# Fourteen of 22 pairs of activation tiles in the down projection by seven products instead of plain ones, in two groups of seven pairs

## The chip, the cores and the metric

The kernel runs on one core of a Trainium2 chip. The metric is the device time of one execution in microseconds; lower is better. The times named are medians of several runs, and the profile comes from one further execution.

## The reference

One encoder layer over two requests of 256 tokens each (512 tokens, 2048 features), in float32: a mixer of neighbourhood attention and a gated delta rule, then a gated feed-forward network, then a last RMS norm. The change is in the feed-forward network's last product:

```python
h = h + mixed
hn = rmsnorm(h, norm_ffn_w)
return h + (jax.nn.silu(hn @ w_gate) * (hn @ w_up)) @ w_down
```

`w_gate` and `w_up` are 2048 x 5632, `w_down` is 5632 x 2048. The 5632 inner features are 44 tiles of 128, or 22 pairs.

## The kernel before

**Precision.** A float32 operand is split in a high and a low part (`split`, L125 on): ScalarE copies the high part (L130), VectorE subtracts it (L131). A plain product is three matmuls of 512 columns: high by high, high by low, low by high (`mm3`).

**Gate and up, by seven products.** `block` (L964) makes a 2 x 2 block of output tiles: two tiles of features by two halves of tokens, from two halves of the inner dimension. It computes Strassen's seven products instead of eight. Each product (L933) runs over 8 tiles of the inner dimension with two matmuls each, one of 512 columns (the high weight by the high and the low part of 256 tokens) and one of 256 (the low weight by the high part). The combinations of activations are made once, ahead of the stage, and lie in the seven slots of `XC`. The combinations of weights are made per block: `second` is w12 + w22 and `first` is w11 + w12, each loaded by SP and then added to by an accumulating DMA on GpSimd's queue (`plus`, L960). `first` is split for the third product; then VectorE adds b22 (L1010) and it is split for the fifth; then VectorE adds b21 (L1022) and it is split for the seventh. `b11`, `b21` and `b22` are loaded again by themselves. The split weights `hi` and `lo` have three buffers, so a split runs up to two products ahead. The pools of `first` and `second` are `gA` for a gate block and `gB` for an up block, one buffer each. The results of the seven products are summed by VectorE from PSUM. After each pair of blocks the activations go to DRAM (`s_act`, L1063), except for the pairs of one segment, which stay on chip in `sA`.

**Down, plain.** A segment is two pairs, four tiles of the inner dimension. `load_act` (L1083) reads a pair of activation tiles from `s_act` and splits it. `down` (L1091) runs, for each of 8 output columns of 256 features, over the segments of a group of tiles on chip: 24 matmuls of 512 columns per segment and column, and at the end VectorE adds PSUM into the residual stream `hT` (L1102), which has been loaded whole from `s_h2`. The segments go in groups: 9 (from `sA`), then 0 to 2, then 3, 4, 5 and 10, then 6 and 7. The last segment, 8, runs by halves of tokens with the final norm beside it (`finish`, `final_norm`).

**Order.** A scheduler orders the instructions of the engines other than TensorE by its own costs; TensorE keeps the order of the program. `high_priority(offset=...)` lets loads and splits be placed ahead. Each engine runs its queue in order, and so do SP and GpSimd with the DMAs that they issue.

Of the kernel before, what the change touches and what calls it, by code (L numbers as in the profile page):

```python
# [18 lines left out]
P = 128  # L19
# [13 lines left out]
FIRST_SEG = 9  # L33
# [32 lines left out]
def hybrid_encoder(ctx: ExitStack, tc: tile.TileContext, xT, w_in, w_ba, w_out, w_gate,  # L66
                   w_up, w_down, nw_mix, nw_ffn, nw_fin, na_bias, conv_w, lane_par,
# [865 lines left out]
    def product(ps, w, c, first, done=False):  # L933

        wh, wl = w
        for k in range(8):
            mm(ps, wh[:, k], XC[k][:, c], start=(first and k == 0), stop=False,
               skip_group_check=True)
            mm(ps[:, 0], wl[:, k], XC[k][:, c, 0], start=False, stop=(done and k == 7),
               skip_group_check=True)  # L940
# [10 lines left out]
    def w_split(src):  # L951
        hi = wp.tile([P, 8, P], F32R, tag="hi", bufs=3, name="w_hi")
        lo = wp.tile([P, 8, P], F32R, tag="lo", bufs=3, name="w_lo")
        split(hi, lo, src)
        return hi, lo
# [8 lines left out]
    def block(src, f, pool, new_out, opened=None):  # L964


        with tc.high_priority(offset=3 * AHEAD):
            first = pool.tile([P, 8, P], F32, tag="first", name="w_first")
            second = pool.tile([P, 8, P], F32, tag="second", name="w_second")
            nc.sync.dma_start(second, src[f + 1, 0])  # L970
            nc.sync.dma_start(first, src[f, 0])
            plus(second, src[f + 1, 1])
            plus(first, src[f + 1, 0])
            b11, b21, b22 = [wp.tile([P, 8, P], F32, tag="raw", bufs=3, name=nm)
                             for nm in ("b11", "b21", "b22")]
            nc.sync.dma_start(b11, src[f, 0])
            nc.sync.dma_start(b21, src[f, 1])
            nc.sync.dma_start(b22, src[f + 1, 1])
# [8 lines left out]
        product(pa, w, A11, True)  # L987
# [3 lines left out]
        p1 = gA.tile([P, L], F32, tag="p1", name="p1")  # L991
# [3 lines left out]
        product(pc, w, S3, True)  # L995
# [4 lines left out]
        product(pd, w, S1, True)  # L1000
        if opened:
            token_rstd2()
        d = fp.tile([P, 2, L], F32, tag="d", name="d")
        tt(d, pd, p7, ALU.subtract)
        with ahead():
            w = w_split(b21)
        product(pa, w, A12, False, True)
# [4 lines left out]
        product(pb, w, S2, True, True)  # L1012
        u2 = fp.tile([P, L], F32, tag="u2", name="u2")
        plus_both(u2, p1, pb)
        tt(out[:, 3], d[:, 0], u2, ALU.subtract)
        tt(out[:, 3], out[:, 3], d[:, 1], ALU.add)
        with ahead():
            w = w_split(b22)
        product(pd, w, S4, False, True)
# [4 lines left out]
        product(pc, w, A22, False, True)  # L1024
        plus_both(out[:, 1], u2, pc)
        a = out.rearrange("p (f b) t -> p f (b t)", f=2)
        tt(a, a, state["rstd2"][:, None, :].broadcast_to([P, 2, T]), ALU.mult)
        return out

# [7 lines left out]
    def open_gate():  # L1037
# [3 lines left out]
                                                 reuse_waits="tile"))  # L1041
        state["gb_cm"] = tc.tile_pool(name="gB", bufs=1, side="right", reuse_waits="tile")
# [3 lines left out]
        state["sA"] = sA_pool.tile([P, 2, SEG, T], F32R, tag="sA", name="aA")  # L1046

    for p in range(NPAIR):
        g4 = block(w_gate, 2 * p, gA,
                   lambda: state["fp"].tile([P, 4, L], F32, tag="g4", name="ga"),  # L1050
                   open_gate if p == 0 else None)
        act(out=g4, in_=g4, func=AF.Silu)
        u4 = block(w_up, 2 * p, state["gB"],
                   lambda: state["fp"].tile([P, 4, L], F32, tag="u4", bufs=2, name="up"))
# [26 lines left out]
    qp = ctx.enter_context(tc.tile_pool(name="qp", bufs=1, side="right", reuse_waits="tile"))  # L1081

    def load_act(s, a):  # L1083

        for i in range(2):
            raw = fp.tile([P, 2 * T], F32, tag="raw_a", name="raw_a")
            nc.gpsimd.dma_start(raw, s_act[2 * s + i])
            split(a[:, 0, 2 * i:2 * i + 2].rearrange("p k t -> p (k t)"),
                  a[:, 1, 2 * i:2 * i + 2].rearrange("p k t -> p (k t)"), raw)

    def down(segs):  # L1091
        for j in range(8):
            ps = [pg.tile([P, T], F32, tag="g", name="ps_g"), sm_tile()]
            for n, (s, a) in enumerate(segs):
                wh, wl = load_w(w_down[s, j], [2, SEG, P])
                for i in range(2):
                    for k in range(SEG):
                        mm3(ps[i], wh[:, i, k], wl[:, i, k], a[:, 0, k], a[:, 1, k],
                            n == 0 and k == 0, n == len(segs) - 1 and k == SEG - 1)
            for i in range(2):  # L1100
                hk = hrow(2 * j + i)
                tt(hk, hk, ps[i], ALU.add)  # L1102

    def down_half(s, aseg, t0, t1, keep):
        for j in range(8):
            wh, wl = keep[0][:, j], keep[1][:, j]
            if t0 == 0:
                load_w(w_down[s, j], [2, SEG, P], (wh, wl))
# [9 lines left out]
    def final_norm(b, acc):  # L1118
# [8 lines left out]
        dgs = fp.tile([P, 2, P], F32, tag="raw_a", name="dgs")  # L1127
# [5 lines left out]
        yo = qp.tile([P, KT, L], F32, tag=f"q{b}", name="yo")  # L1133
        for k, n in ((0, 2), (2, 2), (4, 4), (8, 4), (12, 4)):
            tt(yo[:, k:k + n], hT[k // 8][:, k % 8:k % 8 + n, t0:t1],
               rs[:, None, :].broadcast_to([P, n, L]), ALU.mult)
            nc.sync.dma_start(y[b, k // 4, :, k % 4:k % 4 + n], yo[:, k:k + n])
# [115 lines left out]
```

## Time and profile before

| | |
|---|---|
| median of 3 runs | 2338.44 us (2337.36 to 2339.56) |
| the profiled execution | 2336.3 us, its span 2334.4 us |
| granted TensorE clock | 0.998 |
| TensorE busy | 2301.2 us, 99% of the span |
| VectorE, ScalarE, GpSimd busy | 69%, 42%, 9% |
| DMA | 371.08 MB, mean 159 GB/s |

The gate and up blocks end at about 1839 us of the span; the down projection and the final norm fill the rest. The busy time of an engine says how long it had work in flight. A wait is read from the chain of waits and from the bracket at the end of a timeline row, which gives the idle time before an instruction and what ended it.

### The profile page before, as it was taken

The numbers are of one execution on the slowest core, as the hardware profiler recorded it, in microseconds if no ns is written. First come the engines' busy times: TensorE is split into PE (matmuls) and PEld (weight loads), VectorE is DVE, ScalarE is ACT, GpSimd is POOL, SyncE is SP. The second block draws the span as 40 slices with busy tenths as digits, with TensorE's granted clock in tenths as the row PEclk, the third lists the DMA queues.
The fourth block names the chain that finished last, engine by engine and source line by source line (L and its number), as shares of the span: only waits on it lengthen the run. The fifth ranks groups of instructions, "written<-read, shape, count | busy, mean of one in ns | idle before, by whom it ended". The sixth has DMA issues, their size and how long they took to land.

```text
span 2334.4 us, 31279 instructions
## 1 busy us (share of the span) xinstructions
PE 2301.2 (99%) x12092; PEld 1929.3 (83%) x12092; DVE 1615.1 (69%) x2380; ACT 982.7 (42%) x1478; POOL 218.2 (9%) x326
## 2 busy tenths in 40 slices
PE   9999999999999999999999999999999999999998
PEld 7887788888778788888888888888888888888887
DVE  7744799974666636888888888888888753422346
ACT  6777333324333324644444444444444342311225
POOL 2211100011100011100010101010100110000000
PEclk9999999999999999999999999999999999999999
DMA  5434423265434554777777777767676562422231
GB/s 203 133 118 140 121 93 104 95 143 168 127 118 136 193 168 171 219 187 197 202 191 212 190 210 186 218 184 215 184 203 180 208 224 92 135 99 95 95 126 73
DMA packets 105012, 371.08 MB, mean 159 GB/s; under 512 B 13568, under 2 KB 14032, under 8 KB 103584
## 3 DMA queue, kind: packets, MB, share of 16 engines
q1 hardware_dynamic: 74960, 268.21, 33.9%
q0 software_dynamic: 29904, 100.88, 19.2%
q8 instruction: 95, 1.56, 0.3%
q14 instruction: 53, 0.43, 0.1%
HBM read 333.57 MB, written 35.47 MB: 158 GB/s over the span
## 4 chain that ended last, share of the span: by engine, by line
PE 84%; DVE 8%; ACT 4%; issue 2%; DMA 1%; POOL 0%; SPq 0%; DVEq 0%; ACTq 0%; POOLq 0%
PE ps_g L78 33%; PE ps_s L78 12%; PE ps_a L78 11%; PE ps_c L78 11%; PE ps_d L78 10%; PE ps_b L78 5%; DVE w_lo L131 2%; PE ps_o L78 1%; DVE cacc L335 1%; ACT w_hi L130 1%; DVE prod L546 1%; DVE W L548 1%; ACT E L453 1%; PE ps_s L81 1%; ACT E L455 1%
## 5 line engine op out<-in xcount | busy, mean ns | idle before, releaser
L131 DVE TENSOR_TENSOR w_lo<-w_raw,w_hi 128x1024 fp32r<-128x1024 f32 x222 | 271.2, 1223 | 288.4 <-ACT w_hi L130 285.1
L130 ACT ACTIVATE w_hi<-w_raw 128x1024 fp32r<-128x1024 f32 x222 | 234.1, 1057 | 511.3 <-PE ps_s L78 281.7
L78 PE MATMUL ps_g<-xhi,w_hi 128*128 128x512 f32 x896 | 361.6, 404 | 1.4 <-DVE on L423 1.4
L78 PE MATMUL ps_g<-xhi,w_lo 128*128 128x512 f32 x896 | 350.5, 391 | 2.5 <-DVE w_lo L131 2.5
L78 PE MATMUL ps_g<-xlo,w_hi 128*128 128x512 f32 x896 | 350.2, 391 | 0.5 <-DVE xlo L239 0.5
L78 PE MATMUL ps_a<-xc,w_hi 128*128 128x512 f32 x704 | 252.5, 399 | 2.0 <-DVE p L946 1.2
L78 PE MATMUL ps_d<-xc,w_hi 128*128 128x512 f32 x704 | 250.4, 396 | 1.1 <-ACT w_hi L130 1.1
L78 PE MATMUL ps_c<-xc,w_hi 128*128 128x512 f32 x704 | 250.3, 396 | 0.0
L130 ACT ACTIVATE w_hi<-w_first 128x1024 fp32r<-128x1024 f32 x132 | 140.1, 1061 | 204.6 <-PE ps_c L78 109.5
L130 ACT ACTIVATE w_hi<-b 128x1024 fp32r<-128x1024 f32 x132 | 140.2, 1062 | 193.4 <-issue 115.6
L131 DVE TENSOR_TENSOR w_lo<-w_first,w_hi 128x1024 fp32r<-128x1024 f32 x132 | 161.7, 1225 | 75.0 <-ACT w_hi L130 70.9
L78 PEld LDWEIGHTS ps_g<-xhi,w_lo 128*128 128x128 f32 x896 | 168.3, 188 | 39.7 <-DVE w_lo L131 3.9
L78 PEld LDWEIGHTS ps_g<-xhi,w_hi 128*128 128x128 f32 x896 | 168.6, 188 | 38.6 <-issue 5.7
L78 PE MATMUL ps_a<-xc,w_lo 128*128 128x256 f32 x704 | 197.4, 280 | 0.0
L78 PE MATMUL ps_d<-xc,w_lo 128*128 128x256 f32 x704 | 197.3, 280 | 0.0
L78 PE MATMUL ps_c<-xc,w_lo 128*128 128x256 f32 x704 | 197.3, 280 | 0.0
L78 PEld LDWEIGHTS ps_g<-xlo,w_hi 128*128 128x128 f32 x896 | 168.7, 188 | 34.1 <-DVE xlo L239 1.5
L131 DVE TENSOR_TENSOR w_lo<-b,w_hi 128x1024 fp32r<-128x1024 f32 x132 | 161.2, 1221 | 7.6 <-ACT w_hi L130 0.3
L78 PEld LDWEIGHTS ps_a<-xc,w_hi 128*128 128x128 f32 x704 | 132.1, 188 | 38.1 <-issue 5.9
L78 PEld LDWEIGHTS ps_d<-xc,w_hi 128*128 128x128 f32 x704 | 132.1, 188 | 32.6 <-ACT w_hi L130 1.4
L78 PEld LDWEIGHTS ps_c<-xc,w_hi 128*128 128x128 f32 x704 | 132.1, 188 | 31.2
L78 PEld LDWEIGHTS ps_a<-xc,w_lo 128*128 128x128 f32 x704 | 133.1, 189 | 0.3 <-issue 0.2
(336 smaller groups left out, 4312.0 us busy)
## 6 DMA issues: line engine op xcount, KB each, us to landing
w_raw<-in_w_in_dram SPq DMA_DIRECT2D x110, 512.0 KB, 3.5
w_raw<-in_w_down_dram SPq DMA_DIRECT2D x88, 512.0 KB, 3.3
b<-in_w_gate_dram SPq DMA_DIRECT2D x66, 512.0 KB, 4.1
b<-in_w_up_dram SPq DMA_DIRECT2D x66, 512.0 KB, 6.5
w_raw<-in_w_out_dram SPq DMA_DIRECT2D x32, 512.0 KB, 3.5
w_second<-in_w_gate_dram SPq DMA_DIRECT2D x22, 512.0 KB, 8.4
w_first<-in_w_gate_dram SPq DMA_DIRECT2D x22, 512.0 KB, 6.0
w_second<-in_w_gate_dram POOLq DMA_DIRECT2D x22, 512.0 KB, 5.5
```

The lines of the kernel that those rows point to most:

```text
L78: pin(nc.tensor.matmul(*a, **k))
L81: pin(nc.tensor.transpose(*a))
L130: act(out=hi, in_=src, func=AF.Copy)
L131: tt(lo, src, r32(hi), ALU.subtract)
L335: stt(a3[:, :, lo:hi], x3[:, :, lo + o:hi + o], cw[:, ct, j:j + 1], a3[:, :, lo:hi], ALU.mult, ALU.add)
L453: pin(act(out=E[half[0], s, s:], in_=G[half[0], s:], func=AF.Exp, bias=NG[half[0], s:s + 1]))
L455: pin(act(out=E[half[1], s, :s + 1], in_=G[half[1], :s + 1], func=AF.Exp, bias=NG[half[1], s:s + 1]))
L546: tt(pv, W[:, s0:s1, s0:c], kkq[:, c, 0, None, s0:c].broadcast_to([P, n, j]), ALU.mult)
L548: nc.vector.tensor_reduce(W[:, s0:s1, c], pv, AX.X, ALU.add)
```

## The change

The 44 tiles of the down projection are divided anew. Tiles 0 to 27, 14 pairs, form two groups of seven pairs. Each group is multiplied by `block`, now with 7 tiles of the inner dimension in each half instead of 8: the first tiles of the pairs are one half, the second tiles the other. The other four segments stay plain and run one at a time: 9, then the first group, 7, the second group, 8, and 10 by halves at the end.

The combinations of activations for a group, `XD` (seven tiles of seven slots), are made by `combine` from one loaded pair each, one beside each output column of the plain segment that stands ahead of the group. `hT` is no longer loaded whole: in the first segment ScalarE copies PSUM into it, and an accumulating DMA adds `s_h2`. The results of a group's block are added into `hT` by VectorE (L1149 after). All tiles of a group's blocks come from the pool `fq` with one buffer per tag; loaded pairs, combinations and the blocks' outputs share a ring of three buffers. `w_group` holds the weights of the groups.

```diff
+GROUP = 7
+NGROUP = 2
+FIRST_SEG, MID_SEG, LAST_SEGS = 9, 7, (8, 10)
...
-    def block(src, f, pool, new_out, opened=None):
+    def block(w4, pool, xc, ix, p1_pool, new_out, opened=None):
+        n = len(xc)
+        w11, w21, w12, w22 = w4
         with tc.high_priority(offset=3 * AHEAD):
-            first = pool.tile([P, 8, P], F32, tag="first", name="w_first")
-            second = pool.tile([P, 8, P], F32, tag="second", name="w_second")
+            first = pool.tile([P, n, P], F32, tag="first", name="w_first")
+            second = pool.tile([P, n, P], F32, tag="second", name="w_second")
...
-        d = fp.tile([P, 2, L], F32, tag="d", name="d")
-        tt(d, pd, p7, ALU.subtract)
+        tt(p7, pd, p7, ALU.subtract)
...
-        a = out.rearrange("p (f b) t -> p f (b t)", f=2)
-        tt(a, a, state["rstd2"][:, None, :].broadcast_to([P, 2, T]), ALU.mult)
         return out
...
-    for i in range(KT):
-        nc.gpsimd.dma_start(hrow(i), s_h2[i])
-    fp = ctx.enter_context(tc.tile_pool(name="fq", bufs=2, side="left", reuse_waits="tile"))
+    fq = ctx.enter_context(tc.tile_pool(name="fq", bufs=1, side="right", reuse_waits="tile"))
+    XD = [hq.tile([P, 7, 2, L], F32R, tag=f"xd{k}", name="xd") for k in range(GROUP)]
+    ix = (0, 3, 4, 1, 5, 6, 2)
+
+    def ring(shape, nm):
+        return fq.tile([P] + shape, F32, tag="ra", bufs=3, name=nm)
+
+    def combine(p, k):
+        raw, cm, x = ring([4, L], "raw_a"), ring([4, L], "cmd"), XD[k]
+        nc.gpsimd.dma_start(raw.rearrange("p a t -> p (a t)"), s_act[p])
+        tt(cm[:, :2], raw[:, :2], raw[:, 1:4:2], ALU.subtract)
+        tt(cm[:, 2], cm[:, 1], raw[:, 0], ALU.subtract)
+        tt(cm[:, 3], raw[:, 2], cm[:, 2], ALU.add)
+        split(x[:, 0, 0], x[:, 0, 1], raw[:, 0])
+        split(x[:, 1:3, 0], x[:, 1:3, 1], raw[:, 2:])
+        split(x[:, 3:, 0], x[:, 3:, 1], cm)
...
-    def down(segs):
+    def down(s, a, beside=None, first=False):
         for j in range(8):
+            if beside is not None and j < GROUP:
+                combine(beside + j, j)
...
             for i in range(2):
                 hk = hrow(2 * j + i)
-                tt(hk, hk, ps[i], ALU.add)
+                if first:
+                    nc.scalar.copy(hk, ps[i])
+                else:
+                    tt(hk, hk, ps[i], ALU.add)
+            if first:
+                plus(hcol(j), s_h2[2 * j:2 * j + 2].rearrange("i p t -> p i t"))
+
+    def down_group(g):
+        for j in range(8):
+            out = block([w_group[g, j, i] for i in range(4)], fq, XD, ix, fq,
+                        lambda: ring([4, L], "out"))
+            h4 = hcol(j).rearrange("p i t -> p (i t)")
+            tt(h4, h4, out.rearrange("p a t -> p (a t)"), ALU.add)
...
+            yo = out[:, k:k + n] if b else ring([n, L], "yo")
...
+    down(FIRST_SEG, state["sA"], 0, True)
+    a = load_act(MID_SEG, state["new_sA"]())
+    down_group(0)
+    down(MID_SEG, a, GROUP)
+    a = load_act(LAST_SEGS[0], state["new_sA"]())
+    down_group(1)
...
+    down(LAST_SEGS[0], a)
     for b in range(NB):
-        finish(*groups[-1][0], b, keep)
+        finish(LAST_SEGS[1], last, b, keep)
```

What stands on the queues. On SP before, in the gate and up stage (`b` are the blocks' single weights, gate and up in turn, `first` and `second` each from the pool of its own kind):

```order
L976 DMA b_15344<-in_w_gate_dram 128x1024
L970 DMA w_second<-in_w_up_dram 128x1024
L977 DMA b_15345<-in_w_gate_dram 128x1024
L978 DMA b_15346<-in_w_gate_dram 128x1024
L971 DMA w_first<-in_w_up_dram 128x1024
L976 DMA b_15523<-in_w_up_dram 128x1024
L970 DMA w_second<-in_w_gate_dram 128x1024
```

A block's b21 and b22 stand here between the loads of `second` and `first` of the block after it. On SP after, in the first group:

```order
L983 DMA b_16576<-in_w_group_dram 128x896
L977 DMA w_second<-in_w_group_dram 128x896
L984 DMA b_16577<-in_w_group_dram 128x896
L985 DMA b_16578<-in_w_group_dram 128x896
L978 DMA w_first<-in_w_group_dram 128x896
L983 DMA b_16739<-in_w_group_dram 128x896
L977 DMA w_second<-in_w_group_dram 128x896
```

The five loads are now of one and the same block (b_16576 to b_16578), `first` as the last of them. It goes into the one buffer that the block ahead of it used.

On VectorE after, in the first group, from the third product's split of `first` to the seventh's (`p_16605` is p1, `p_16626` p7; b_16577 is b21 and b_16578 b22):

```order
L135 TENSOR_TENSOR w_lo<-w_first,w_hi 128x896
L135 TENSOR_TENSOR w_lo<-b_16577,w_hi 128x896
L1016 TENSOR_TENSOR w_first<-w_first,b_16578 128x896
L950 TENSOR_TENSOR p_16605<-p_16605,ps_a 128x256
L135 TENSOR_TENSOR w_lo<-w_first,w_hi 128x896
L1010 TENSOR_TENSOR p_16626<-ps_d,p_16626 128x512
L1028 TENSOR_TENSOR w_first<-w_first,b_16577 128x896
L135 TENSOR_TENSOR w_lo<-b_16578,w_hi 128x896
L135 TENSOR_TENSOR w_lo<-w_first,w_hi 128x896
```

The same stretch before, of a gate block (`p_15734` is p1, `d` the difference that p7 now holds itself):

```order
L131 TENSOR_TENSOR w_lo<-w_first,w_hi 128x1024
L1027 TENSOR_TENSOR up<-up,rstd_8231 128x1024
L1010 TENSOR_TENSOR w_first<-w_first,b_15705 128x1024
L131 TENSOR_TENSOR w_lo<-b_15704,w_hi 128x1024
L1055 TENSOR_TENSOR up<-up,ga 128x1024
L131 TENSOR_TENSOR w_lo<-w_first,w_hi 128x1024
L946 TENSOR_TENSOR p_15734<-p_15734,ps_a 128x256
L1022 TENSOR_TENSOR w_first<-w_first,b_15704 128x1024
L131 TENSOR_TENSOR w_lo<-b_15705,w_hi 128x1024
L1004 TENSOR_TENSOR d<-ps_d,p_15757 128x512
L131 TENSOR_TENSOR w_lo<-w_first,w_hi 128x1024
```

The passes over the weights are the same seven; the multiplications by `rstd` and by the gate have gone from among them, and a pass has 896 elements instead of 1024.

On GpSimd's queue before, from the end of the gate and up stage (`s_h` is the stored residual stream):

```order
L1063 DMA s_act<-up 128x1024
L1079 DMA hT_16063<-s_h_103 128x512 x7
L1063 DMA s_act<-up 128x1024
L1079 DMA hT_16063<-s_h_103 128x512
L1079 DMA hT_16064<-s_h_103 128x512 x8
L1087 DMA raw_a<-s_act 128x1024 x20
```

and after:

```order
L1074 DMA s_act<-up 128x1024 x2
L967 DMA hT_16019<-s_h_103 128x2x512
L1107 DMA raw_a<-s_act 128x1024
L967 DMA hT_16019<-s_h_103 128x2x512
L967 DMA w_second<-in_w_group_dram 128x896
L967 DMA w_first<-in_w_group_dram 128x896
L1107 DMA raw_a<-s_act 128x1024
L967 DMA hT_16019<-s_h_103 128x2x512
L1107 DMA raw_a<-s_act 128x1024
L967 DMA hT_16019<-s_h_103 128x2x512
```

The loads of pairs for the combinations (`raw_a`) now stand between accumulates into hT, each of which follows the copies of one output column, and the second of them behind the accumulates of the first block's two sums.

More of the change, by code (lines that the diff above doesn't have):

```diff
@@ L928, in hybrid_encoder, with product @@
             tt(acc, acc, sq, ALU.add)
[L933 removed]
+    def product(ps, w, xc, c, first, done=False):
         wh, wl = w
[L936 to L937 removed]
+        for k, x in enumerate(xc):
+            mm(ps, wh[:, k], x[:, c], start=(first and k == 0), stop=False,
                skip_group_check=True)
[L939 removed]
+            mm(ps[:, 0], wl[:, k], x[:, c, 0], start=False, stop=(done and k == len(xc) - 1),
                skip_group_check=True)
@@ L986, in block @@
             w = w_split(b11)
-        product(pa, w, A11, True)
+        product(pa, w, xc, ix[A11], True)
         if opened:
```

126 lines of the change are left out of this document (65 added, 61 removed).

## The prediction

> **What bounds the kernel now.** I read the page's engine line first, then the table of stretches for the two stages that the change joins, then the chain of waits.
>
> ```profile
> PE 2301.2 (99%) x12092; PEld 1929.3 (83%) x12092; DVE 1615.1 (69%) x2380; ACT 982.7 (42%) x1478; POOL 218.2 (9%) x326
> 1413.60:1808.08 394.48, 394.12 (x2241) 341.71 (x2241) 338.95 (x433) 179.66 (x213) 39.83 (x49) 1.00 0.73 197
> 1855.69:2264.01 408.32, 408.29 (x1802) 337.93 (x1801) 155.77 (x154) 102.24 (x98) 9.51 (x18) 1.00 0.38 126
> ```
>
> The second line is a stretch of gate and up blocks (seven products each), the third a stretch of the plain down projection; behind the length stand the busy times of PE, weight load, VectorE, ScalarE and GpSimd, then the clock, the DMA share and GB/s. TensorE never waits in either, at full clock. So a fewer-columns change is worth its full TensorE time, as long as nothing starves TensorE. The two stages differ in what stands behind TensorE: in the blocks VectorE is busy 338.95 of 394.48 us (86%) and the DMA engines 0.73; in the plain stage VectorE is at 38% and the DMA engines at 0.38.
>
> The chain of waits gives the pace inside a block:
>
> ```profile
> 1413.60 3.02 PE ps_a L78 x16
> 1416.62 2.77 PE ps_b L78 x16
> 1419.39 2.77 PE ps_d L78 x16
> 1422.17 2.77 PE ps_c L78 x16
> 1424.94 2.77 PE ps_a L78 x16
> ```
>
> A product is 16 matmuls, 2.77 us, with a somewhat longer one now and then, and one product follows the other at once. 2241 matmuls are 20 blocks of 112, so a block takes 394.48/20 = 19.72 us.
>
> **What goes and what comes on TensorE.** A group's block has 14 matmuls to a product, of the same two shapes, so 14/16 of 19.72 = 17.26 us, and 2.47 us to a product. Sixteen blocks: 276.1 us. They replace seven plain segments of 192 matmuls; a plain matmul is 408.32/1802 = 0.2266 us, a segment 43.5 us, seven 304.5. Gain 28.4 us (26 to 31, with the product at 2.77 throughout or at 2.83). This is the gain if TensorE never waits.
>
> **The new wait: one buffer for the sum of weights.** In the gate and up stage `first` and `second` come from two pools in turn, so a sum has a whole other block in which to be built. The groups take both from `fq`, one buffer each. `first` is needed for the third product, then gets b22 and b21 added, and its last split, for the seventh product, frees it. Only then can SP load the next block's w11 into it, and after that GpSimd add w12. In the trace this refill is seen in full. First VectorE's timeline in an up block, up to the release:
>
> ```profile
> 1504.22 1.23 DVE L131 TENSOR_TENSOR w_lo<-w_first,w_hi 128x1024 fp32r<-128x1024 f32 x1
> 1505.37 1.22 DVE L1027 TENSOR_TENSOR ga<-ga,rstd 128x1024 f32<-128x1024 f32 x1
> 1506.50 1.22 DVE L1010 TENSOR_TENSOR w_first<-w_first,b 128x1024 f32<-128x1024 f32 x1
> 1507.63 1.22 DVE L131 TENSOR_TENSOR w_lo<-b,w_hi 128x1024 fp32r<-128x1024 f32 x1
> 1508.77 0.42 DVE L946 TENSOR_TENSOR p<-p,ps_a 128x256 f32<-128x256 f32 x1
> 1509.82 1.22 DVE L131 TENSOR_TENSOR w_lo<-w_first,w_hi 128x1024 fp32r<-128x1024 f32 x1 [0.63 <-ACT w_hi L130]
> ...
> 1512.22 0.68 DVE L1004 TENSOR_TENSOR d<-ps_d,p 128x512 f32<-128x512 f32 x1
> 1512.82 1.21 DVE L131 TENSOR_TENSOR w_lo<-b,w_hi 128x1024 fp32r<-128x1024 f32 x1
> 1515.37 1.23 DVE L131 TENSOR_TENSOR w_lo<-w_first,w_hi 128x1024 fp32r<-128x1024 f32 x1 [1.33 <-ACT w_hi L130]
> ```
>
> SP's queue from there on:
>
> ```profile
> 1516.62 0.33 SPq L971 DMA_DIRECT2D w_first<-in_w_up_dram  x1
> 1519.39 0.33 SPq L976 DMA_DIRECT2D b<-in_w_up_dram  x1
> 1522.12 0.33 SPq L970 DMA_DIRECT2D w_second<-in_w_gate_dram  x1
> ```
>
> On GpSimd's queue, the accumulate for that load; and the table of DMA issues, with the median time from issue to landing in the last column:
>
> ```profile
> 1521.39 0.86 POOL L962 DMA_DIRECT2D w_first<-in_w_up_dram  x1 [13.49 <-DVE up L949]
> ```
>
> ```profile
> w_raw<-in_w_down_dram SPq DMA_DIRECT2D x88, 512.0 KB, 3.3
> w_first<-in_w_gate_dram SPq DMA_DIRECT2D x22, 512.0 KB, 6.0
> w_first<-in_w_gate_dram POOLq DMA_DIRECT2D x22, 512.0 KB, 6.7
> w_first<-in_w_up_dram SPq DMA_DIRECT2D x22, 512.0 KB, 4.3
> w_second<-in_w_up_dram POOLq DMA_DIRECT2D x22, 512.0 KB, 5.6
> w_first<-in_w_up_dram POOLq DMA_DIRECT2D x22, 512.0 KB, 8.9
> raw_a<-s_act POOLq DMA_DIRECT2D x20, 512.0 KB, 4.3
> ```
>
> The last pass over `first` ends at 1516.60, SP issues the load 0.02 us later, GpSimd the accumulate 4.77 us after that, and it lands 8.9 us on (median): 13.7 us of refill, hidden because the next up block starts two blocks later. In a group there is one block less of cover.
>
> How long is `first` held? I count from the moment R at which it is whole, if everything waits for it. The table of groups has ScalarE's split of 1024 elements at 1.06 us and its copy of 512 at 0.57 (and VectorE's add into hT, used further down):
>
> ```profile
> L130 ACT ACTIVATE w_hi<-w_first 128x1024 fp32r<-128x1024 f32 x66 | 70.0, 1061 | 102.5 <-PE ps_c L78 55.1 <-PE ps_a L78 33.3 <-DVE d L1004 7.7
> L997 ACT COPY p<-ps_c 128x512 f32<-128x512 f32 x22 | 12.5, 567 | 0.0
> L1102 DVE TENSOR_TENSOR hT<-hT,ps_s 128x512 f32<-128x512 f32 x28 | 19.2, 686 | 42.7 <-PE ps_s L78 42.7
> ```
>
> So 896 take 0.94. VectorE's queue then holds, in order: split of `first`, split of b21, add b22, the small p1 add, split of `first`, the p7 subtraction, add b21, split of b22, last split of `first`. Seven of these are passes of 896; a full pass follows another in 1.14 us above (1505.37, 1506.50, 1507.63), so 1.0 for 896. With the two small ones (0.42 and 0.60), 0.6 of waiting for ScalarE in the middle as in the row at 1509.82, and the tail of the last pass: 0.98 + 7.0 + 1.0 + 0.6 + 0.1 = 9.7 us. TensorE would allow it by 9.1 (third product from R + 2.0, fourth ends at R + 6.9, then the split, 2.2), so VectorE decides.
>
> A block's period is then 9.7 us plus the refill, if that is more than 17.26: there is room for a refill of 7.5 us. Ends for the refill at 7 tiles instead of 8: quickest, an undisturbed load (3.3), hand-off to GpSimd (0.5, what 4.77 leaves beyond a load of 4.3), the quicker accumulates (5.6), less 0.5 for the smaller tiles: 8.9. Slowest, as the 13.7 above. I take 11.7, near the slow rows: in a group the loads of the following b11 and second fall just before and just after the accumulate's issue, as they stand around 1521.39 here (1519.39 and 1522.12); less the smaller tiles, and without the writes of activations that pass there. Behind the waiting load on SP stand only b11 and second of the block after, behind the accumulate on GpSimd the next second: none is due within 10 us. Behind the waiting split on ScalarE stand the split of b21 and the copies of p1 and p7, on VectorE the passes counted above: they wait too, and are in the 9.7. Period 9.7 + 11.7 = 21.4, a wait of 4.1 us for every block but the first of a group: 14 x 4.1 = 58 us (ends 1.3 and 6.1 a block, 19 and 86).
>
> The Trainium skill, page "DMA: Bandwidth & Descriptors", section "Anatomy of one DMA — SWDGE (gpsimd) path", fits a DMA as 2.0 us plus bytes over 436 GB/s: 3.05 us for 448 KB. By that the refill would be 6.6 us, inside the room, and the wait nothing; every row above is slower than it at 512 KB.
>
> **The combinations beside the plain products.** They must be whole before a group's first product. In the first plain segment, GpSimd's queue has the loads of pairs between accumulates into hT that wait for TensorE, and the second pair's load stands behind the accumulate of `first`, whose load stands on SP behind the seventh weight tile of the segment:
>
> ```profile
> 1839.35 2.75 PE ps_g L78 x12
> ...
> 1846.97 0.33 SPq L138 DMA_DIRECT2D w_raw<-in_w_down_dram  x1
> ```
>
> The first row is the chain of waits at the segment's start, 1839.3; the second, SP's queue, has that tile going out 7.7 us later. With 0.7 for the two issues behind it, 6.0 for the load of `first`, 0.5 and 0.9 for hand-off and issue, the second pair's load goes out at 16 and lands at 21 (4.3 in the row of raw_a, and 0.5). A combination costs VectorE 0.68 + 3 x 0.42 + 0.68 + 1.22 = 3.8 us, about 5 with the weight split between and its waits for ScalarE; six more end at 51, where TensorE wants the last at 43.5 + 2 = 45.5. So 5.5 us, from 0 to 11. In the second such segment everything is loaded, and VectorE is the limit: 3.8 + 1.2 + 2 x 0.69 = 6.4 us beside a step of 5.44, less in part for the overlap of its passes: 2 us (0 to 5). Together 8.
>
> **Edits that I cost at nothing.** The p7 subtraction in place: p7's last reader is the fifth product's sum, its next writer the second product of the next block. The copies of PSUM into hT by ScalarE instead of VectorE's adds: ScalarE is busy 102.24 of 408.32 us there (16 x 0.57 = 9 us if it were full). The output through the ring and sA: up to 2 us if a write holds a buffer, hidden for the first half by the second half's products.
>
> **Sum.** −28.4 + 58 + 8 = +37.6 us on the profiled execution of 2336.3 us (span 2334.4): 2373.9. That execution is 2.1 us under the median 2338.4, so I forecast 2376.
>
> **Rivals.**
>
> The refill at its quickest rows (8.9 us): period 18.6, 14 x 1.3 = 19; with 3 for the starts, −28.4 + 22 = −6: 2332, just faster. For it: the loads of the next block could pass before or after the accumulate. Against it: they are released by the splits that follow the last one of `first`, so they come just then. 0.16.
>
> The refill fits its 7.5 us: only the starts are left, −28.4 + 8 = −20: 2318. It decides from a load and an accumulate that land in 7.0 us together; the quickest medians make 8.9 at 512 KB. This is also what the fit of the Trainium skill gives. 0.07.
>
> The combinations bind instead: if each pair's load waits for the combination before it, a combination takes 4.3 + 5 = 9.3 us and seven 65, 20 us late before each group. With the wait for `first` beside it: −28.4 + 58 + 40 = +70: 2408. Against it: three ring buffers let a second load run ahead. 0.12.
>
> **How the numbers follow.** The forecast, slower by 15 to 60 us, gets 0.57, the quick refill 0.16, the fitting one 0.07, the bound combinations 0.12, and 0.08 is left for results between the first rival and the forecast. About what a measurement of this kernel can tell from no change is 0.2%, 4.7 us. Faster: 0.16 + 0.07 less 0.03 of the first rival that falls within 4.7 us, 0.20. Same: that 0.03 and 0.05 of what is left, 0.08. Slower: 0.57 + 0.12 + 0.03, 0.72. The range takes in the quick refill and the upper ends: 2330 to 2410; the forecast's own is 2353 to 2398.
>
> **What would show it.** Right: TensorE idle before the third product of each block but the first, released by a split of `first` that waited for its DMA; blocks some 21 us apart; the SP issue of `first` to its landing by GpSimd 11 to 13 us; some us of idle time at each group's first product, released by the combinations. Wrong: blocks at 17.3 us with no idle time (then the refill was mis-sized or is not in series with the last split), or the idle time at the starts of the groups alone.

## The result, and the profile after it

| | before | changed |
|---|---|---|
| median of the runs | 2338.37 us (2337.36 to 2339.56) | 2399.11 us (2398.23 to 2401.62) |
| ratio to before | 1 | 1.0258, 95% interval 1.0245 to 1.0271 |
| profiled execution, span | 2336.3 us, 2334.4 us | 2399.09 us, 2397.3 us |
| mean granted TensorE clock, whole span | 0.998 | 0.981 |

The change costs 61 us. The forecast was 2376 with a range of 2330 to 2410, so sign and range held. The sum is 23 us short, and the forecast's own narrower range, 2353 to 2398, ended just below the measured time.

The page of the changed kernel: the busy time of each engine, then the chain that ended last, by engine. The last row is that chain before the change.

```profile
PE 2307.9 (96%) x12316; PEld 1937.9 (81%) x12316; DVE 1795.6 (75%) x2698; ACT 1066.1 (44%) x1626; POOL 247.1 (10%) x350
PE 69%; DVE 12%; DMA 8%; ACT 5%; issue 4%; POOL 0%; SPq 0%; ACTq 0%; DVEq 0%; POOLq 0%
PE 84%; DVE 8%; ACT 4%; issue 2%; DMA 1%; POOL 0%; SPq 0%; DVEq 0%; ACTq 0%; POOLq 0%
```

TensorE's busy time did not fall, although it has fewer columns to stream: it rose from 2301.2 to 2307.9 us. That is a first hint that it was slowed, not only made to wait. In the chain VectorE has grown from 8% to 12% and the DMA engines from 1% to 8%.

The table of stretches for the new stage: the first plain segment, group 0 cut into its first block and the seven others, and group 1 cut in the same way. Behind the length stand the busy times of PE, weight load, VectorE, ScalarE and GpSimd, then clock, DMA share and GB/s.

```profile
1837.10:1880.63 43.53, 43.53 (x194) 36.04 (x193) 23.73 (x34) 19.81 (x30) 11.21 (x13) 1.00 0.92 249
1880.63:1917.89 37.26, 22.50 (x100) 18.05 (x98) 28.44 (x41) 18.72 (x28) 7.73 (x9) 0.77 0.75 192
1917.89:2075.14 157.25, 134.63 (x688) 113.33 (x687) 105.25 (x147) 53.82 (x72) 11.97 (x15) 0.91 0.59 147
2118.70:2137.24 18.54, 17.36 (x99) 14.90 (x98) 16.82 (x23) 9.47 (x12) 1.52 (x2) 1.00 0.56 153
2137.24:2293.26 156.02, 135.08 (x688) 113.63 (x687) 106.49 (x147) 53.02 (x70) 11.65 (x15) 0.91 0.57 144
```

The sixteen blocks take 37.26 + 157.25 + 18.54 + 156.02 = 369.07 us in place of the 304.5 of seven plain segments, which is 64.6 us more; the gate and up stage ended 2.1 us earlier than before, and the spans differ by 62.9. The other fourteen blocks take 22.4 us each on average, at a clock of 0.91, and all but one of them have the wait that is shown next. Group 0's first block is a case of its own.

TensorE's waits in the two groups: on what, how long in all, how often, the longest.

```profile
PE ps_d L82 <- ACT w_hi L134: 36.0, 13, 4.7
PE ps_a L82 <- DVE xd L135: 12.8, 3, 6.7
PE ps_d L82 <- DVE w_lo L135: 7.6, 14, 0.6
```

`ps_d` is the third product's bank, so the first and third row are the waits for the split of `first` that were named in the forecast; the second is group 0's start. The chain of waits through one turn of the loop, with the rows that carry it:

```profile
1932.33 4.35 DMA w_first<-in_w_group_dram
...
1937.21 7.28 DMA w_first<-in_w_group_dram
...
1944.59 0.96 ACT w_hi L134
...
1945.57 1.10 DVE w_lo L135
...
1946.71 4.42 PE ps_d L82 x13
1951.13 3.13 PE ps_a L82 x13
...
1954.34 0.96 ACT w_hi L134
...
1955.33 1.09 DVE w_lo L135
...
1956.45 4.04 DMA w_first<-in_w_group_dram
```

Read from top to bottom: load of `first`, accumulate, split, then two products of TensorE, the last split, and the next load 0.03 us behind it. The refill is 1944.48 − 1932.33 = 12.2 us (forecast 11.7). The hold, from there to the next load, is 12.0 us (forecast 9.7), and what lengthens it are two products that take 4.4 and 3.1 us in the chain (13 of the 14 matmuls of each) instead of 2.47. Three neighbouring stretches say why; they are the wait, the third product and the fourth:

```profile
1939.20:1945.59 6.39, 2.63 (x17) 2.03 (x15) 0.02 (x1) 1.00 (x2) 0.85 (x1) 1.00 0.79 144
1945.59:1950.93 5.34, 4.77 (x14) 3.82 (x15) 4.50 (x5) 2.48 (x4) 0.00 (x0) 0.53 0.23 45
1950.93:1954.20 3.27, 3.27 (x15) 2.80 (x15) 2.69 (x3) 0.95 (x1) 0.00 (x0) 0.73 0.09 19
```

After 6.39 − 2.63 = 3.8 us of idle time TensorE resumes at a granted clock of 0.53 and is back at full speed only two products later. The forecast had no such term.

### The profile page after: what moved, and what is told of

Read it like the earlier page. It is cut to its first block, busy times and chain, and to the rows that moved or that the text cites. A ratio compares the mean times of both kernels' runs of the same rounds, so it can differ in the third digit from the quotient of the medians.

```text
span 2397.3 us, 32437 instructions
## 1 busy us (share of the span) xinstructions
PE 2307.9 (96%) x12316; PEld 1937.9 (81%) x12316; DVE 1795.6 (75%) x2698; ACT 1066.1 (44%) x1626; POOL 247.1 (10%) x350
## 4 chain that ended last, share of the span: by engine, by line
PE 69%; DVE 12%; DMA 8%; ACT 5%; issue 4%; POOL 0%; SPq 0%; ACTq 0%; DVEq 0%; POOLq 0%
PE ps_g L82 24%; PE ps_d L82 12%; PE ps_a L82 12%; PE ps_c L82 10%; DMA w_first<-in_w_group_dram 6%; PE ps_b L82 5%; DVE w_lo L135 4%; PE ps_s L82 4%; ACT w_hi L134 2%; DMA raw_a<-s_act 2%; PE ps_o L82 1%; DVE cacc L339 1%; DVE prod L550 1%; ACT E L457 1%; DVE W L552 1%
## 5 line engine op out<-in xcount | busy, mean ns | idle before, releaser
L134 ACT ACTIVATE w_hi<-w_first 128x1024 fp32r<-128x1024 f32 (+1 forms) x180 | 186.0, 1033 | 364.4 <-DMA w_first<-in_w_group_dram 112.4
L135 DVE TENSOR_TENSOR w_lo<-w_first,w_hi 128x1024 fp32r<-128x1024 f32 (+1 forms) x180 | 214.0, 1189 | 166.4 <-ACT w_hi L134 162.1
L135 DVE TENSOR_TENSOR w_lo<-w_raw,w_hi 128x1024 fp32r<-128x1024 f32 x166 | 202.9, 1223 | 120.2 <-ACT w_hi L134 115.6
L134 ACT ACTIVATE w_hi<-w_raw 128x1024 fp32r<-128x1024 f32 x166 | 175.3, 1058 | 263.2 <-PE ps_g L82 218.2
L134 ACT ACTIVATE w_hi<-b 128x1024 fp32r<-128x1024 f32 (+1 forms) x180 | 186.0, 1033 | 221.5 <-issue 133.4
L135 DVE TENSOR_TENSOR w_lo<-b,w_hi 128x1024 fp32r<-128x1024 f32 (+1 forms) x180 | 213.5, 1186 | 8.8 <-ACT w_hi L134 2.9
L82 PE MATMUL ps_d<-xd,w_hi 128*128 128x512 f32 x224 | 100.2, 472 | 37.8 <-ACT w_hi L134 36.0
```

What stands on the lines that cost most here:

```text
L82: pin(nc.tensor.matmul(*a, **k))
L134: act(out=hi, in_=src, func=AF.Copy)
L135: tt(lo, src, r32(hi), ALU.subtract)
```

## The experiments

The theory after the result (A): `first` has one buffer, so its refill stands in series with its release; the wait that follows lowers TensorE's clock, which lengthens the hold (A'); and group 0 starts late because its raw loads share the DMA engines (S). The rivals: contention of the DMA engines wherever the load is issued (C), the pass that makes `w_lo` as the cause of the slow products (D), VectorE's work on the combinations (V), GpSimd's queue (Q). Ratios are to the kernel before, run on the same chip.

**1 and 2. Two buffers of `first`.** Room for the second buffer is made in the groups alone: p7 lies in two quarters of the output tile, and u2 in p1.

```
-            first = pool.tile([P, n, P], F32, tag="first", name="w_first")
+            first = pool.tile([P, n, P], F32, tag="first", bufs=2 if n == GROUP else 1, ...)
-        p7 = fp.tile([P, 2, L], F32, tag="p7", name="p7")
+        p7 = out[:, 1:3] if n == GROUP else fp.tile(...)
-        u2 = fp.tile([P, L], F32, tag="u2", name="u2")
+        u2 = p1 if n == GROUP else fp.tile(...)
```

The second kernel gives the load and the accumulate of `first` a higher priority besides, in the gate and up blocks too.

> The groups' `first` gets two buffers (p7 lies in the output tile and u2 in p1, in the groups alone, to make room); in SP's queue its load still stands right behind that of b22, which waits for b22's own last split. Theory A, the refill in series with the release of `first` and its place in SP's queue: the load can go out only as early as b22's load does, 2.0 to 2.5 us earlier than before (in the changed kernel's queue b22 went out at 1953.89, `first` at 1956.45), so blocks of some 19.5 us, waits before the third product still there, and 14 x 2.0 to 2.5 = 28 to 35 us less: 2364 to 2371. Rival B, the buffer alone decides: the waits and the slow clock behind them vanish, 2399 - 74 = 2325. Rival C, DMA contention decides, whenever the load is issued: 2395 to 2400.

> Two buffers of `first` as in the run before, and the load of the next sum placed in SP's queue ahead of the following block's b11, so that it has a whole block to land. Theory A: no wait before the third product from the second block on, the granted clock back at 1.0 in those blocks, blocks at 17.1 to 17.5 us; what is left of the loss is the start of group 0 (some 20 us): 38 us of waits and 36 us of slowed products go, 2320 to 2330, which is faster than the kernel before (2338). Rival C, DMA contention decides: 2390 to 2400, with the accumulates simply landing later. Rival D, the slow third and fourth products are not due to the wait but to the pass that makes w_lo: waits go, the products stay slow, some 2360.

Measured: 2329.94 us, ratio 0.9961 (0.9947 to 0.9975), and with the priority 2334.6, ratio 0.9982 (0.9972 to 0.9992). The stretches of the first of the two: group 0's first block, its other seven, and the last seven of group 1.

```profile
1883.31:1921.31 38.00, 23.17 (x99) 18.58 (x98) 28.37 (x41) 18.84 (x28) 7.72 (x9) 0.73 0.79 201
1921.31:2042.51 121.20, 121.20 (x688) 105.06 (x687) 105.04 (x147) 54.87 (x72) 11.62 (x14) 1.00 0.74 188
2108.13:2227.03 118.90, 118.90 (x688) 103.96 (x687) 106.02 (x148) 53.93 (x70) 10.58 (x13) 1.00 0.69 181
```

No idle time and a clock of 1.00 in the fourteen blocks, which take 17.31 and 16.99 us. DMA share and GB/s have gone up, from 0.59 and 147 to 0.74 and 188, so C has fallen: the DMA engines had room. My expectation for the first run went wrong in its premise. The load of `first` does stand right behind that of b22 in SP's queue, but with two buffers it is the sum for the block after next:

```profile
1931.23 0.33 SPq L986 DMA_DIRECT2D b<-in_w_group_dram  x1
1933.45 0.33 SPq L979 DMA_DIRECT2D w_first<-in_w_group_dram  x1
```

The block that begins at 1938.63 already has its sum; this one is for the block at 1955.94. So the order gave a block of lead without the priority, and the second run is near to a repetition of the first. It does not tell A from B, which make the same of that order; both say that one buffer cost the 14 waits.

**3. The moved tiles alone, and the changed kernel once more.** The control has the p7 and u2 lines of above, and `first` with one buffer.

> The control: p7 in the output tile and u2 in p1 for the groups, as in the runs with two buffers, but `first` with one buffer. Theory A (the single buffer costs the time): no change from the changed kernel, 2395 to 2403. Rival: the moved tiles themselves brought the gain (other waits of VectorE): 2340 or less.

> The changed kernel itself, so that the control with moved tiles alone (2388) has its partner on a chip of these runs. If the moved tiles did nothing: 2386 to 2391, and the difference was the chip; if they shortened some waits: 2396 to 2402.

Measured: 2388.39, ratio 1.0218 (1.0204 to 1.0232); the changed kernel again 2396.78, ratio 1.0251 (1.0230 to 1.0273). The control came out below its 2395 to 2403, and the repeat where the expectation had put tiles that shorten some waits (2396 to 2402). The control's interval lies below that of the first measurement (1.0245 to 1.0271) and just touches that of the repeat, so moving the tiles is probably worth some 8 to 11 us of the 69; by which waits I did not trace. The other 58 us, from 2388.39 to 2329.94, are the buffer's.

**4. The wait kept, TensorE kept busy in it.**

```
+        if n == GROUP:
+            for _ in range(20):
+                mm(pb[...][:, :256], idle[:, :P], idle[:, :256], start=True, stop=True, ...)
         product(pd, w, xc, ix[S1], True)
```

> Between the second and third product of each group block TensorE gets 20 matmuls of 128x256 bf16 (some 2.2 to 2.7 us at the 0.11 to 0.135 us of the 56 at the kernel's start) into a bank that the fifth product overwrites; nothing else changes, so the single buffer and its wait stay. Theory A': the slow third product (4.5 to 5.3 us at a granted clock of 0.53 to 0.66) comes from the idle time ahead of it; with TensorE at work the third product takes 2.5 to 3.5 us at a clock of 0.9 or more, the hold of `first` shortens with it, blocks fall from 21.7 to some 19.5 us: 2360 to 2375. Rival D, the product waits for w_lo or the clock falls for another reason: third products stay at 4.5 us or more, and the time is 2395 to 2410.

Measured: 2383.38, ratio 1.0200 (1.0183 to 1.0217). First the stretches of one block, from about the end of its second product: the added matmuls with what is left of the wait, then the third product. The last row is seven blocks of group 0.

```profile
1942.87:1945.73 2.86, 2.36 (x22) 1.87 (x20) 0.02 (x1) 1.00 (x2) 0.73 (x1) 1.00 0.23 47
1945.73:1949.32 3.59, 2.96 (x15) 2.14 (x15) 3.56 (x5) 2.33 (x4) 0.12 (x1) 1.00 0.76 132
1916.73:2064.16 147.43, 141.30 (x828) 118.06 (x827) 106.12 (x147) 53.20 (x72) 12.20 (x15) 1.00 0.64 158
```

The third product takes 3.59 us at a clock of 1.00, where it mostly took 4.5 to 5.35 behind a wait before. Of the 1.1 us that it is over 2.47, 0.63 is the wait for `w_lo` behind its first matmul: so D is right in that part. What a third product took beyond 3.59 us before went with the clock, as A' says; the other 0.5 us of the 1.1 is busy time at full clock, and open. The seven blocks of each group go from 157.25 and 156.02 to 147.43 and 146.45 us: 19.4 us less in all, that is 1.4 a block, and this is the clock's share. (In the repeat of the changed kernel they took 155.00 and 154.88 us, which makes the share 16.0.) The time fell 13 to 16 us where 24 to 39 was expected, because I had put the whole excess of the third product down to the clock, and because the blocks stay bound by the loop. Besides, the first block of group 1 now takes 23.37 us instead of 18.54: it has no wait for `first` to fill. And this kernel shows the loop as the forecast had it, at full clock:

```profile
1932.74 4.41 DMA w_first<-in_w_group_dram
...
1937.68 6.94 DMA w_first<-in_w_group_dram
...
1944.73 0.96 ACT w_hi L134
...
1954.14 4.38 DMA w_first<-in_w_group_dram
```

Refill 1944.62 − 1932.74 = 11.9, hold 9.5, period 21.4 us; the forecast was 11.7, 9.7 and 21.4. In the 9.5 us the chain holds splits by ScalarE and VectorE, sums and a subtraction of VectorE, and no product of TensorE.

**5. No accumulate for `first`** (w12 is missing from that sum in the groups).

```
-            plus(first, w12)
+            if n != GROUP:
+                plus(first, w12)
```

> The groups leave out the accumulate of w12 into `first` (so w12 is missing from that sum); the load alone refills it. Theory A: the refill falls from 12.2 to about 5 us, below the room of 7.5, so the waits go as with two buffers: 2320 to 2335. If the refill's length is in the wait for the load rather than in the accumulate (rival): a gain of a few us a block only, 2360 to 2380.

Measured: 2329.23, ratio 0.9960 (0.9945 to 0.9975). The last seven blocks of group 0:

```profile
1923.58:2042.49 118.91, 118.91 (x689) 104.85 (x687) 105.43 (x147) 54.73 (x72) 6.58 (x8) 1.00 0.63 169
```

16.99 us a block with one buffer: a refill of one load (4.0 us by the changed kernel's table of DMA issues, quoted below) fits the room. Two different edits, one that takes the series away and one that shortens it, end at the same time; the cause of the 14 waits is settled.

**6. The residual's accumulates out of the first plain segment.** On the changed kernel, and on the one with two buffers.

```
-            if first:
-                plus(hcol(j), s_h2[2 * j:2 * j + 2]...)          # in down()
+            if g == 0:
+                plus(hcol(j), s_h2[2 * j:2 * j + 2]...)          # in down_group(), after the block
```

> On the changed kernel alone: the eight accumulates of the residual into hT (512 KB each) leave the first plain segment; each is issued after the block of group 0 that wrote that part of hT. Theory S (the start of group 0 is late because these accumulates share the DMA engines and GpSimd's queue with the raw loads of the combinations): the raw loads land in 4 to 5 us instead of 7.6, the first product of group 0 takes 3 to 8 us instead of 17.2, a gain of 9 to 14 us there, part of it given back by longer refills beside the moved accumulates (0 to 1 us a block): 2383 to 2395. Rival V (VectorE's work on the combinations sets the start): first product still over 14 us, 2397 to 2405.

> Two buffers of `first` and the residual's accumulates moved into group 0. Theory S: the start of group 0 falls from some 23 us (1.6 in the plain segment, 15 before the second product, 6 within the first block) to 6 to 10, and the moved accumulates are hidden, since the refill has a block of lead: 2330 - 13 to 17 = 2313 to 2317. Rival V: within 4 us of the two buffers alone, 2326 to 2333.

Measured: 2388.56, ratio 1.0217 (1.0202 to 1.0233), and with two buffers 2330.51, ratio 0.9965 (0.9952 to 0.9977). The median from issue to landing of the raw loads in the first plain segment and the start of the group, in the changed kernel:

```profile
raw_a<-s_act POOLq DMA_DIRECT2D x7, 512.0 KB, 7.6
```

and with the accumulates moved, on that kernel, with the stretches of the plain segment and of group 0's first block:

```profile
raw_a<-s_act POOLq DMA_DIRECT2D x9, 512.0 KB, 4.7
```

```profile
1837.15:1880.71 43.56, 43.56 (x195) 36.05 (x193) 30.14 (x45) 23.99 (x37) 6.04 (x10) 1.00 0.68 218
1880.71:1910.75 30.04, 20.95 (x100) 17.29 (x98) 21.46 (x30) 14.62 (x21) 2.82 (x4) 0.89 0.49 144
```

The DMA share of the segment falls from 0.92 to 0.68, the loads land in 4.7 us, and group 0's first product takes 5.33 us instead of 17.2 (from one product's first matmul to the next product's): S is right about the first product, V is not. (This profile is of an execution of 2378.97 us, 10 us below the median.) But the first block as a whole only falls from 37.26 to 30.04 us, since its third product now takes 8.46. With two buffers it went likewise: 38.00 to 31.06 us in that block, and 4.6 us given back at the end of group 0. I had expected 2313 to 2317, and the time fell into V's range, 2326 to 2333, though not for V's reason: the gain was eaten by what comes next, in the same block (TensorE waits 5.4 and 4.4 us for VectorE's sum p1 there) and at the end of the group.

**7 and 8. The raw loads on SP's queue,** on the kernel with two buffers, with and without the residual's accumulates moved.

```
-        nc.gpsimd.dma_start(raw.rearrange("p a t -> p (a t)"), s_act[p])
+        nc.sync.dma_start(raw.rearrange("p a t -> p (a t)"), s_act[p])
```

> The same, and the raw loads of the combinations issued from SP's queue instead of GpSimd's. They no longer stand behind accumulates, but SP's loads of b11, b21 and b22 now stand behind raw loads that wait for a ring buffer. Theory S: the loads were late through bandwidth and not through GpSimd's queue, so 0 to 4 us less than the run before: 2309 to 2317. Rival Q (the queue's place decides): over 6 us less if GpSimd's queue was the limit, or 5 to 20 us more if SP's queue now starves the first block.

> Two buffers of `first` and the combinations' raw loads on SP's queue, with the residual's accumulates left beside the first plain segment. It tells which of the two edits gave the 12 us of the run that had both. If the accumulates' share of the DMA engines delays the raw loads, on whichever queue they are issued: the first product of group 0 stays at 13 us or more and the time at 2325 to 2332. If GpSimd's queue was the delay: first product under 10 us, 2316 to 2321.

Measured: both edits 2318.23, ratio 0.9913 (0.9899 to 0.9926); the queue alone 2327.25, ratio 0.9956 (0.9942 to 0.9969). The raw loads and group 0's first block, with the queue alone:

```profile
raw_a<-s_act SPq DMA_DIRECT2D x7, 512.0 KB, 6.3
```

```profile
1880.36:1913.44 33.08, 20.62 (x100) 16.35 (x98) 25.57 (x40) 18.45 (x27) 5.67 (x6) 0.85 0.82 215
```

and with both edits, with the first block of group 1 behind it:

```profile
raw_a<-s_act SPq DMA_DIRECT2D x7, 512.0 KB, 4.6
```

```profile
1882.75:1909.67 26.92, 20.08 (x100) 16.67 (x98) 22.55 (x34) 14.54 (x21) 2.00 (x4) 0.87 0.53 159
2074.40:2092.22 17.82, 17.54 (x99) 14.98 (x98) 16.18 (x22) 9.45 (x12) 1.74 (x2) 1.00 0.53 157
```

The queue alone takes group 0's first product from 17.40 to 13.75 us, and S had expected 13 or more. On SP's queue no accumulate stands ahead of the raw loads, and moving the accumulates still takes that product from 13.75 to 8.29 us: so their share of the DMA engines delays the loads by itself, and by more than the queue did. Together with the moved accumulates the queue is worth 12 us more than those alone. S had allowed 4, and it is twice what Q needed, but not where Q looked for it: 4.1 us in group 0's first block, 4.6 at that group's end, 3.8 in group 1's first block (21.62 to 17.82). Why the last two come out better I did not test. This is the fastest kernel of the study, 20 us below the kernel before.

**9. The next segment's activations loaded later,** written ahead of the third block of each group instead of ahead of the first, with two buffers, the accumulates in group 0, and the raw loads on SP's and on GpSimd's queue.

```
-    a = load_act(MID_SEG, state["new_sA"]())
-    down_group(0)
+    a = down_group(0, MID_SEG)         # which calls load_act at j == 2; group 1 likewise
```

> Two buffers of `first`, the residual's accumulates in group 0, the raw loads on SP's queue, and the next plain segment's activations loaded from the third block of each group on instead of ahead of it. In the run before this, ScalarE and VectorE stood 3.7 us in group 0's first block at the split of those activations, whose load had not landed, with the split of `first` and the sum p1 behind it. Theory: that block's third product falls from 4.5 to 2.5-3.5 us and the second from 4.2 to about 3, 2318 - 3 to 6 = 2312 to 2315, what is left being the first product's wait (8.3 against 2.5). Rival: the splits were waiting for VectorE's combinations anyway, 2316 to 2320.

> As the run before, but with the combinations' raw loads left on GpSimd's queue. There the first block lost 5 us at the third product and 1.6 at the fourth, where PE waited for VectorE's sum p1 behind the split of the late activations, and group 1's first block as much. If that split is the cause and not the queue: 2330 - 8 to 14 = 2316 to 2322, close to the run with SP. If GpSimd's queue itself is the limit (raw loads behind accumulates that wait): 2325 to 2331.

Measured: 2324.19, ratio 0.9943 (0.9931 to 0.9955), and 2333.99, ratio 0.9982 (0.9971 to 0.9993). With SP's queue it is slower than without the edit; with GpSimd's it is no faster, as the intervals (0.9971 to 0.9993 and 0.9952 to 0.9977) overlap. My theory fell. ScalarE's wait in the first block before the edit, and the one in the second block after it, both with SP's queue:

```profile
ACT aA L134 <- DMA raw_a<-s_act: 3.7, 1, 3.7
```

```profile
ACT aA L134 <- DMA raw_a<-s_act: 10.4, 1, 10.4
```

The first block did get better: its third product is back at 2.43 us. But ScalarE reaches the split of those activations again before their load has landed, now beside one of the moved accumulates, and stands 10.4 us with the split of `first` behind it. The edit moved load and split together, so the split still stood in ScalarE's queue ahead of the landing. A split placed later than its load was not tried.

## Why the prediction came out as it did

The undisturbed blocks of experiment 1 are the measure: 8 x 17.31 + 8 x 16.99 = 274.4 us.

| step of the prediction | forecast | measured |
|---|---|---|
| fewer columns, TensorE never waiting | −28.4 | 274.4 − 304.5 = −30.1 |
| wait for the single buffer, 14 blocks, at full clock | +58 | 147.43 + 146.45 − 240.1 = +53.8 |
| clock lowered by those waits | not there | 313.3 − 293.9 = +19.4 |
| group 0's start | +5.5 | 37.26 − 17.31 = +20.0 |
| group 1's start | +2 | 18.54 − 16.99 = +1.6 |
| gate and up stage | 0 | −2.1 |
| sum (the starts rounded to 8 in the forecast) | +37.6 | +62.6 (spans: +62.9) |

240.1 us are the fourteen undisturbed blocks (121.20 + 118.90), 313.3 the same in the changed kernel, 293.9 with TensorE kept busy. In the changed kernel itself the 73.2 us over 240.1 are 43.6 of idle time and 29.6 of longer products; at full clock more of them would have been idle time.

**The gain and the loop.** Right in mechanism, place and size, though the ends of the gain should have been 27 and 33 us: 112 products of 14/16 of 2.83 or 2.77. The wait stands before the third product, released by the split of `first`, and with the clock at 1.00 the loop runs 21.4 us of which the refill is 11.9 and VectorE's hold 9.5. The choice near the slow rows for the refill (between 8.9 and 13.7) was the right one. The accumulate's own median is shown by the table of DMA issues of the changed kernel, with the load above it:

```profile
w_first<-in_w_group_dram SPq DMA_DIRECT2D x16, 448.0 KB, 4.0
w_first<-in_w_group_dram POOLq DMA_DIRECT2D x16, 448.0 KB, 7.1
```

With the 0.5 us of hand-off these make 11.6. The rivals of a refill that fits or almost fits are out, and the 6.6 us by the fit of the Trainium skill, page "DMA: Bandwidth & Descriptors", with them: the accumulate of `first`, 448 KB, takes 7.1 us where it gives 3.05.

**What the sum lacked.** The step "TensorE would allow it by 9.1 … so VectorE decides" took the products behind the wait at 2.47 us, and so did the period. The rows of before that the prediction reads could not show otherwise, because in its gate, up and plain stages TensorE never waits and the clock is 1.00. But that trace has one place that does, ahead of these stages: from 783.78 to 787.20 us TensorE is busy for 0.67 us only, and for the next 3.41 us the granted clock is 0.50. The Trainium skill, page "TensorE: Matmul & The Clock Gate", section "HAM oscillation — how this bites in real kernels", warns of exactly this: a loop that waits for a DMA over 3.4 us on every turn starts every turn at half clock. A forecast wait of 4.1 us was over that figure and should have been weighed by it. In the section "What's actually happening" of that page the Trainium skill gives some 3.4 us of sustained work until the full clock is back; half of that for 14 waits would be 24 us, an estimate from that page, near the 16.0 to 19.4 measured.

**The term that was mis-sized.** The start of group 0 was put at 5.5 us, from a raw load that takes 4.3 us and combinations of 5 us each. Its raw loads took 7.6, at a DMA share of 0.92, because I counted the accumulates into hT as instructions that stand between them in GpSimd's queue and not as 4 MB that pass at the same time. VectorE's timeline has the first pass over the last pair but one, and the last pass of the last:

```profile
1890.14 0.69 DVE L1108 TENSOR_TENSOR cmd<-raw_a 128x512 f32<-128x512 f32 x1 [2.67 <-DMA raw_a<-s_act]
...
1899.86 1.22 DVE L135 TENSOR_TENSOR xd<-cmd,xd 128x1024 fp32r<-128x1024 f32 x1
```

VectorE stood idle for a load at 1890, which is when I had the last combination done (51 us behind 1839.3); it ended at 1901.1. TensorE took 17.2 us instead of 2.47 for the first product, and the products behind it, at a mean clock of 0.77 in that block, make up the rest of the 20. The rival of combinations that bind gave 20 us for a group: near in size for group 0, but by loads that wait for combinations and not for the DMA engines, and wrong for group 1, where everything was loaded. So it is chance that the measured 2399 lies nearer to that rival's 2408 than to the forecast.

The start of group 1 is near its forecast by chance too. Its first product took 2.46 us, with no wait for combinations; the 1.6 us are mostly one wait of 1.2 us behind the third product, for the sum p1 of VectorE.

## What to carry to other kernels

A buffer that is released late and refilled by two DMAs in a row is a loop of its own: add hold and refill, and compare with the block's time before counting columns saved. When the loop is longer, price the wait twice, once as idle time and once for the slower clock that can follow it. Of a DMA that is moved into a busy stage count the bytes as well as the place in the queue, and look for the split or copy that reaches its engine's queue before the data has landed, since that is what makes a late load everybody's wait.

## What the runs showed of the hardware

How short an idle time lowers TensorE's clock was not expected. Two waits of the changed kernel, each with the third product behind it:

```profile
2139.67:2144.38 4.71, 2.59 (x17) 2.01 (x15) 0.02 (x1) 1.00 (x2) 0.39 (x1) 1.00 0.59 153
2144.38:2147.97 3.59, 2.96 (x15) 2.14 (x15) 3.56 (x5) 2.32 (x4) 0.46 (x1) 1.00 0.70 112
2274.80:2278.55 3.75, 2.59 (x17) 2.03 (x15) 0.02 (x1) 1.00 (x2) 0.55 (x1) 1.00 0.88 282
2278.55:2283.32 4.77, 4.14 (x14) 3.29 (x15) 4.70 (x6) 2.47 (x4) 0.00 (x0) 0.69 0.06 24
```

Behind 4.71 − 2.59 = 2.1 us of idle time the clock stayed at 1.00, behind 1.2 us it fell to 0.69. Over the five kernels with one buffer and an accumulate, the waits before a third product sort as follows (without the first blocks of the groups): up to 1.12 us none lowered the clock of the third product, between 1.16 and 2.75 us 20 of 25 did, and from 2.92 us on all 21; the lowest mean over a third product is 0.50.

What decides is where the idle time falls. In the clock records of the fourteen traces the clock is either 1.00 or 0.50, and in each trace all its falls lie on one grid of 3.413 us. The same two waits, with the stretches of that grid:

```profile
2140.45:2143.86 3.41, 1.81 (x11) 1.31 (x9) 0.00 (x0) 0.48 (x1) 0.00 (x0) 1.00 0.61 158
2143.86:2147.28 3.42, 2.28 (x11) 1.78 (x12) 2.89 (x3) 2.15 (x4) 0.85 (x1) 1.00 0.52 75
...
2276.98:2280.40 3.42, 1.63 (x8) 0.96 (x7) 1.84 (x2) 2.05 (x3) 0.00 (x0) 1.00 0.46 162
2280.40:2283.81 3.41, 3.41 (x13) 2.82 (x12) 3.38 (x5) 1.84 (x3) 0.00 (x0) 0.50 0.00 0
```

The longer wait lies across two stretches, which have 1.60 and 1.14 us of idle time, and the clock stays. The shorter one lies in one stretch, together with 0.63 us inside the third product; that stretch has 1.79 us of idle time, and the next one runs at 0.50. Counted over all fourteen traces, a stretch at full clock with up to 1.55 us of idle time was followed by half clock in 0 of 9280 cases (190 of them with 0.5 us or more), one with 1.91 us or more in all 84, and of the 32 between them in 17. So in these runs about half a stretch of idle time is enough. The Trainium skill, page "TensorE: Matmul & The Clock Gate", section "What's actually happening", gives half clock after an idle window of about 3.4 us, and windows that run on freely. The 0.50 and the grid agree with it; that a window must be idle as a whole, if the page is read so, does not agree with 1.79 us in one, and here the runs decide.
